# A hybrid encoder layer on one Trainium2 core: fewer accumulating bias transfers at the end, and earlier requests at the start of the last stage

## The chip, the cores and the metric

The kernel runs on one core of one Trainium2 chip. The metric is the device time of one execution in microseconds (us). Within the core, TensorE (PE in the profile) multiplies matrices, VectorE (DVE) and ScalarE (ACT) work elementwise, and GpSimd (POOL) and SyncE (SP) mostly ask for transfers. All transfers run on the same sixteen DMA engines.

## The reference

One layer over a sequence of 512 tokens of width 2048, in float32. The attention in the middle is not touched by the change; what follows it is.

```python
h = jnp.einsum('bsd,de->bse', x, w_in[layer])
qa, ka, va, ga, qb, kb, vb, gb = jnp.split(h, splits, axis=-1)
ya = _dilated_attention(heads(qa, N_HEADS_A), heads(ka, N_HEADS_A), heads(va, N_HEADS_A), t5_bias)
yb = _neighbourhood_attention(heads(qb, N_HEADS_B), heads(kb, N_HEADS_B), heads(vb, N_HEADS_B), na_rpb[layer])
ya = merge(ya) * jax.nn.silu(ga.astype(jnp.float32))
yb = merge(yb) * jax.nn.silu(gb.astype(jnp.float32))
y = jnp.concatenate([ya, yb], axis=-1).astype(x.dtype)
out = jnp.einsum('bse,ed->bsd', y, w_out[layer])
x = _layer_norm(DEEPNORM_ALPHA * x + out, ln_gain[layer], ln_bias[layer])
```

`_layer_norm` subtracts the mean over the 2048 columns, divides by the square root of the variance plus 1e-5, multiplies by the gain and adds the bias.

## The kernel before

Every float32 product is made of three matmuls: a high part (`wh`, made by ScalarE) and a low part (`wl`, the rest, made by VectorE) of the weights, and the same two parts of the data. The first two of the three use `wh`, the third `wl`.

The program has three stages. First the input projection in blocks. Then the attention over 32 heads in steps n = 0 to 131 (four steps a head): `scores`, an `exponent` on ScalarE, and two steps later `turn`, which transposes the probabilities p on TensorE and splits them into `th` (ScalarE) and `tl` (VectorE); `values` multiplies them with v. `fill` puts matmuls of the gates and of half the output projection between them. Last comes the rest of the output projection, as a list of 40 jobs, which `project(n)` works off. A job is twelve matmuls, mostly on one 128x1024 weight piece. `project(n)` also makes the high part (`high`, L898) and the low part (`low`, L903) of the weight of job n + 2, and runs the functions that `at(n, ...)` put down for job n, in the order in which they were put down. Jobs -2 and -1 are in steps 127 and 129 of the attention.

Some of the late products are arranged after Strassen. They need sums of quarters of y: `again(i)` asks in GpSimd's queue for pair i of y from DRAM (`ysum<-y_d`, L974), `combine_y(i)` forms the sums on VectorE (`csum`, L979 to L981), and `high_y` and `low_y` split them one and two jobs later. Two buffers serve in turn, so `again(i)` waits for `combine_y(i - 2)`; the two buffers held biases and probabilities of the heads before. The last pair of y goes through `rc_d` (denominators to DRAM), `rc` (back, spread over the partitions) and a product on VectorE (L779) before it is whole. Product 1 sums into `p1`, product 2 into `p2` and product 3 into `p3`, in the pools `pss` and `pst` of two PSUM banks each, which the attention used for its scores and its transposes.

`last_weight(u)` splits the four weight pieces of the last column block (`wlast`, L88 and L89), which jobs 36 and 38 and the matmuls behind the jobs use. The tokens are four rows t = 0 to 3 of 128, the columns four pieces i = 0 to 3 of 512. `norm(t)` normalises a row t < 3: `centre(i)` on VectorE (L1055) subtracts the mean and multiplies by the gain, `rescale(i)` on ScalarE (L1062) multiplies by the reciprocal root, an accumulating transfer in GpSimd's queue (`z<-in_lbias`, L1063) adds the bias, and SP stores the piece (`out<-z`, L1064) once that transfer has landed. Of the twelve pieces of these rows one (t = 2, i = 3) gets its bias on VectorE from a tile `bb[0]` instead (L1060). `last_norm` handles row 3, with the statistics' part of the shift made by small matmuls, and issues its stores (L1239) from ScalarE and SP in turn. Instructions of an engine and transfers of a queue start in the order in which they were recorded. The order is the program's own in these stages.

Of the kernel before, what the change touches and what calls it, by code (L numbers as in the profile page):

```python
# [9 lines left out]
AF = mybir.ActivationFunctionType  # L10
ALU = mybir.AluOpType
# [48 lines left out]
def _view(t, offset, dims):  # L60
    return bass.AP(tensor=t.tensor, offset=t.offset + offset, ap=dims)
# [10 lines left out]
def hybrid_layer(tc, xT, xn, w_in, w_early, w_mid, w_gate, w_out, t5x, brow, rpb, cmask, eye, gain, lbias, out):  # L72
    nc = tc.nc
    from contextlib import ExitStack
    with ExitStack() as ctx:
# [799 lines left out]
        def at(n, *fns):  # L875
            at_job.setdefault(n, []).extend(fns)

        def fetch(m):
            W[m] = slot(f"t{m % 4}", F32, "lraw") if m % 8 > 3 else raw_ring.next("lraw")
            nc.sync.dma_start(W[m], late_tiles[m])  # L880
# [91 lines left out]
        def again(i):  # L972
            cut_y[i] = yr.next("ysum")[:, :1024].rearrange("p (n q) -> p n q", n=4)
            nc.gpsimd.dma_start(cut_y[i].rearrange("p n q -> p (n q)"), y_d[i].rearrange("p n q -> p (n q)"))  # L974
# [49 lines left out]
            nc.scalar.activation(parts[name][t], acc[t], AF.Copy)  # L1024

        def gains():
            for tiles, src, first, some in ((gb, gain, 0, range(4)), (bb, lbias, 1, (3,))):
                for i in some:
                    t = slot(f"n{first + i}", F32, "gain")
                    nc.sync.dma_start(t, _view(src, 512 * i, [[0, 128], [1, 512]]))  # L1030
                    tiles.append(t)

        def last_weight(u):
            wts[u + 4] = [slot(f"r{2 * u + m}", F32R, "wlast") for m in range(2)]
            split(W[32 + u], *wts[u + 4])
# [12 lines left out]
        def norm(t):  # L1048
            mv = small.tile([128, 2], F32, name="mv", tag="mv")
            rs = small.tile([128, 1], F32, name="rs", tag="rs")  # L1050
            nm = small.tile([128, 1], F32, name="nm", tag="nm")

            def centre(i):
                zt = z[t][i]
                nc.vector.scalar_tensor_tensor(zt, zt, mv[:, 0:1], gb[i], op0=ALU.subtract, op1=ALU.mult)  # L1055

            def rescale(i):
                zt = z[t][i]
                if t == 2 and i == 3:
                    last.append(lambda: nc.vector.scalar_tensor_tensor(zt, zt, rs, bb[0], op0=ALU.mult, op1=ALU.add))  # L1060
                else:
                    nc.scalar.activation(zt, zt, AF.Copy, scale=rs)  # L1062
                    nc.gpsimd.dma_start(zt, _view(lbias, 512 * i, [[0, 128], [1, 512]]), accum_op=ALU.add)  # L1063
                last.append(lambda: nc.sync.dma_start(out[t * 128:t * 128 + 128, 512 * i:512 * i + 512], zt))  # L1064

            nc.vector.bn_aggr(mv, st[t])
            nc.scalar.activation(rs, mv[:, 1:2], AF.Sqrt, bias=eps)
            centre(1)
            nc.vector.reciprocal(rs, rs)
            rescale(1)  # L1070
            for i in (0, 2, 3):
                centre(i)
                rescale(i)
            while last and t < 2:
                last.pop(0)()

        def load_shift():

# [17 lines left out]
                    nc.sync.dma_start(f(rows[c][r:r + 1]), f(parts[:, at_ + 4 * c:at_ + 4 * c + 4]))  # L1096

        accs3, last = {}, []
        p1 = product(1, pss, 0)
        p2 = product(2, pst, 4)  # L1100
        o2 = second_half(2, 8)
        product(6, None, 12, p1)
        p5 = product(5, pacc, 16)
        product(7, None, 20, p1)
        p3 = product(3, pst, 24)
        product(4, None, 28, p1)
        for t in range(2):
            jobs.extend(((None, None, lambda w, t=t: third(t)), (None, None, lambda w: None)))
        for u in range(4):
            at(31 + u, lambda u=u: last_weight(u))  # L1110
        starts = (4, 6, 7, 9, 10, 12, 13, 14)
        for i, n in enumerate(starts):
            at(starts[i - 2] + 1 if i > 1 else 0, lambda i=i: again(i))
        for i, n in enumerate(starts):
            at(n, lambda i=i: combine_y(i))
            at(n + 1, lambda i=i: high_y(i))
# [36 lines left out]
        with tc.manual_schedule(engines=engines):  # L1153
            prepare()
            for _ in range(3):
                close()
            while step[0] < 0:
                fill(7)
                close()
            for n in range(132):  # L1160
                b, i = n % 4, n // 8
                mixing = n % 4 == 2 and 6 <= n <= 130
                amount = ((4, 5, 3, 5) if n < 80 else (4, 4, 3, 4))[b]
                if b == 0 and n < 124:
                    load_bias(n // 4 + 1)
                if n % 8 == 0 and n < 120:
                    load_kq(i + 1)
                if n % 8 == 4 and n < 128:
                    if n < 120:
                        load_v(i + 1)  # L1170
                    load_sg(i)
                exponent = scores(n) if n < 128 else None
                if mixing:
                    if exponent:
                        exponent()
                    behind_min(2)
                    fill(2)
                    mine, theirs, y, t = values(n // 4 - 1)
                    nc.scalar.activation(t, theirs, AF.Copy)
                    nc.vector.tensor_tensor(y, mine, t, ALU.add)  # L1180
                    fill(amount - 2)
                else:
                    fill(2)
                if 2 <= n < 130:
                    turn(n - 2)
                if b == 3:
                    behind_min(2 if len(held) > 3 and held[0][0] > 1 else 1)
                if not mixing:
                    if exponent:
                        exponent()  # L1190
                    fill(amount - 2)
                if n >= 8 and n % 8 == 0:
                    later(0, lambda i=i: nc.vector.reciprocal(dens[i - 1], dens[i - 1]))
                if n >= 8 and n % 8 == 2:
                    share(i - 1)
                if n >= 8 and n % 8 == 4:
                    later(0, lambda i=i: gate(i - 1), 4)
                if n % 8 == 1 and 2 <= i < 2 * PAIRS:
                    gated(i - 2)
                if n % 8 == 7 and i >= 2 * PAIRS - 1:  # L1200
                    gated(i - 1)
                if n >= 80 and n % 4 == 0 and n < 96:
                    load_x((n - 80) // 4)
                if n == 125:
                    while stream:
                        raws.append(raw_ring.next("wraw"))
                        nc.sync.dma_start(raws[-1], stream.pop(0))
                    W.update(enumerate(raws))
                    for m in range(4, 8):
                        fetch(m)  # L1210
                if n in (127, 129):
                    project((n - 131) // 2)
                close()
            fill(400)
            for n in range(len(jobs)):
                project(n)
        def last_norm(rows):
# [35 lines left out]
                nc.tensor.matmul(c, left[0:5], rows[i][0:5], start=True, stop=True)  # L1253
                shifts.append(c)
            centre(3)
            rescale(3, whole, bb[0])
            rescale(2, whole, shifts[0])
            rescale(0, whole, shifts[1])
            for part in (slice(0, 256), slice(256, 512)):
# [90 lines left out]
```

## Time and profile before

| | |
|---|---|
| median of three runs | 980.69 us (980.23 to 981.07) |
| profiled execution, its own time | 981.69 us |
| its span | 979.9 us, granted TensorE clock 0.994 |
| TensorE busy | 957.9 us of the span, 98% |
| VectorE, ScalarE, GpSimd busy | 797.3, 526.1, 234.6 us |
| DMA | 227.75 MB, mean 232 GB/s |
| accumulating bias transfers | 11 of 256 KB, 6.1 us each from issue to landing |
| first and last of them issued | 948.46 and 968.18 us |
| last arithmetic of VectorE ends | 967.40 us |

The span is what the profile covers; the execution's own time holds what lies around it. Times in the trace count from the span's start. Idle time of an engine costs something only where TensorE, or the end of the program, waits for it.

### The profile page before, as it was taken

The page shows a single profiled execution, that of the slowest core. Times are in us where ns is not written, and L with a number is a line of the kernel's source. Part 1 is how long each engine was busy: PE and PEld are TensorE (multiplying, and loading weights), DVE is VectorE, ACT ScalarE, POOL GpSimd, SP SyncE. Part 2 cuts the span into 40 slices and gives each one's busy share as a digit, 9 for nine tenths or more (in the row PEclk, how much of TensorE's full clock was granted, in tenths as well). Part 3 has the DMA queues.
Part 4 walks back from the last instruction along what each step waited for, and adds up shares of the span by engine and source line. Part 5 has one row for each costly group of instructions (what it writes and reads, how often), then busy time and mean ns, then how long its engine had stood idle before and what let it go on. Part 6 is the DMA issues. An engine that isn't in the chain of part 4 may idle for free.

```text
span 979.9 us, 14247 instructions
## 1 busy us (share of the span) xinstructions
PE 957.9 (98%) x4741; PEld 794.4 (81%) x4741; DVE 797.3 (81%) x1219; ACT 526.1 (54%) x900; POOL 234.6 (24%) x418
## 2 busy tenths in 40 slices
PE   8999999999999999999999999999999999999993
PEld 6878888888888889988888888888888778778873
DVE  7897778779789788897899857788878787799784
ACT  7454444444444344444445447777778777554531
POOL 1006646735645111111111100111111101210012
PEclk9999999999999999999999999999999999999997
DMA  9715797698496398743994887788879977677729
GB/s 334 275 65 133 224 322 215 179 292 234 113 361 205 106 345 252 248 172 127 287 254 170 260 274 244 239 257 270 264 233 282 322 254 236 223 249 231 253 36 255
DMA packets 131273, 227.75 MB, mean 232 GB/s; under 512 B 51247, under 2 KB 71599, under 8 KB 131200
## 3 DMA queue, kind: packets, MB, share of 16 engines
q1 hardware_dynamic: 109248, 174.93, 55.1%
q0 software_dynamic: 21232, 51.00, 17.8%
q10 hardware_dynamic: 720, 0.92, 0.3%
q8 instruction: 37, 0.61, 0.3%
q14 instruction: 36, 0.29, 0.1%
HBM read 169.66 MB, written 57.08 MB: 231 GB/s over the span
## 4 chain that ended last, share of the span: by engine, by line
PE 86%; issue 6%; DMA 3%; DVE 2%; ACT 1%; POOL 1%; POOLq 0%; SPq 0%; DVEq 0%; ACTq 0%
PE acc L405 16%; PE acc L407 16%; PE acc L406 16%; PE acc L601 9%; PE acc L924 5%; PE acc L807 5%; PE pt L726 3%; PE pv L748 3%; DMA rc_d<-tmp 2%; PE sc L707 2%; PE sc L706 2%; PE pt L262 1%; PE acc L281 1%; PE acc L283 1%; PE acc L282 1%
## 5 line engine op out<-in xcount | busy, mean ns | idle before, releaser
L378 ACT ACTIVATE wh<-braw 128x1024 fp32r<-128x1024 f32 x182 | 193.2, 1062 | 267.8 <-PE acc L406 198.2
L383 DVE TENSOR_TENSOR wl<-braw,wh 128x1024 fp32r<-128x1024 f32 x182 | 223.1, 1228 | 41.4 <-ACT wh L378 41.3
L405 PE MATMUL acc<-wh,xk 128*128 128x512 f32 x384 | 151.3, 394 | 0.0
L407 PE MATMUL acc<-wl,xk 128*128 128x512 f32 x384 | 149.7, 390 | 0.0
L406 PE MATMUL acc<-wh,xk 128*128 128x512 f32 x384 | 149.5, 389 | 0.0
L374 DVE TENSOR_TENSOR braw<-braw 128x1024 f32<-128x1024 f32 x104 | 127.6, 1227 | 0.1
L405 PE MATMUL acc<-wh,op 128*128 128x512 f32 x288 | 113.1, 393 | 0.0
L407 PE MATMUL acc<-wl,op 128*128 128x512 f32 x288 | 112.2, 390 | 0.0
L406 PE MATMUL acc<-wh,op 128*128 128x512 f32 x288 | 112.1, 389 | 0.0
L732 DVE TENSOR_TENSOR tl<-pt,th 128x256 fp32r<-128x256 f32 (+1 forms) x128 | 71.1, 555 | 25.1 <-ACT th L731 22.7
L405 PEld LDWEIGHTS acc<-wh,xk 128*128 128x128 f32 x384 | 72.1, 188 | 15.2 <-ACT bias L153 0.9
L407 PEld LDWEIGHTS acc<-wl,xk 128*128 128x128 f32 x384 | 72.1, 188 | 15.2
L406 PEld LDWEIGHTS acc<-wh,xk 128*128 128x128 f32 x384 | 72.2, 188 | 14.5
L601 PE MATMUL acc<-xk,wh 128*128 128x512 f32 x256 | 80.9, 407 | 0.0
L667 ACT ACTIVATE p<-s,mn 128x512 f32<-128x512 f32 (+1 forms) x96 | 62.4, 649 | 25.7 <-DVE mn L663 25.2
L663 DVE CUSTOM_DVE_ANT_0 s<-sc,biases 128x512 f32<-128x512 f32 (+2 forms) x128 | 67.7, 529 | 9.5 <-PE sc L707 8.8
L731 ACT ACTIVATE th<-pt 128x256 fp32r<-128x256 f32 (+1 forms) x128 | 62.2, 487 | 22.0 <-PE pt L726 19.8
L807 PE MATMUL acc<-wh,yk 128*128 128x512 f32 x192 | 67.8, 404 | 0.0
L163 POOL DMA_DIRECT2D bias<-rows_d x128 | 61.4, 487 | 16.4 <-DMA bias<-rows_d 6.4
L407 PEld LDWEIGHTS acc<-wl,op 128*128 128x128 f32 x288 | 54.1, 188 | 11.4
L406 PEld LDWEIGHTS acc<-wh,op 128*128 128x128 f32 x288 | 54.1, 188 | 11.0
L405 PEld LDWEIGHTS acc<-wh,op 128*128 128x128 f32 x288 | 54.1, 188 | 10.9
(202 smaller groups left out, 1878.9 us busy)
## 6 DMA issues: line engine op xcount, KB each, us to landing
braw<-in_w_in SPq DMA_DIRECT2D x96, 512.0 KB
k_d<-kst SPq DMA_DIRECT2D x64, 128.0 KB
q_d<-kst SPq DMA_DIRECT2D x64, 128.0 KB
v_d<-vst SPq DMA_DIRECT2D x32, 256.0 KB
wsum<-in_w_out POOLq DMA_DIRECT2D x32, 256.0 KB, 4.6
t_d<-wsum POOLq DMA_DIRECT2D x32, 256.0 KB, 3.2
q<-q_d SPq DMA_DIRECT2D x32, 256.0 KB
wraw<-in_w_gate SPq DMA_DIRECT2D x16, 512.0 KB
```

The source lines that it names most:

```text
L374: nc.vector.tensor_tensor(raws[q][u], raws[q][u], raws[other][u], ALU.add)
L378: nc.scalar.activation(h, raws[q][u], AF.Copy)
L383: nc.vector.tensor_tensor(l, raws[q][u], f(h), ALU.subtract)
L405: nc.tensor.matmul(accs[t], ah[:, q], h[:, c], start=first and k == 0, stop=False, skip_group_check=skip)
L406: nc.tensor.matmul(accs[t], al[:, q], h[:, c], start=False, stop=False, skip_group_check=skip)
L407: nc.tensor.matmul(accs[t], ah[:, q], l[:, c], start=False, stop=k == 7, skip_group_check=skip)
L601: nc.tensor.matmul(acc, w[:, k * 128:k * 128 + 128], X[8 * u + k][:, s], start=u == 0 and n == 0 and k == 0, stop=u == 1 and n == 2 and k ...
L663: nc.vector.tensor_tensor_reduce(*flat, bias, 1.0, 3e38, ALU.add, ALU.min, mn)
L667: nc.scalar.activation(p[:, to:to + n].rearrange("p (b r c) -> p b r c", r=8, c=c), s[:, :n].rearrange(order, r=8, c=c), AF.Exp, bias=mn, ...
L731: nc.scalar.activation(th, pt[:, :nch], AF.Copy)
L732: nc.vector.tensor_tensor(tl, pt[:, :nch], f(th), ALU.subtract)
L807: nc.tensor.matmul(acc[:, part], yk[k][:, t // 2, s, c], w[:, wk], start=first and kk == 0 and n == 0, stop=last and kk == 1 and n == 2)
```

## The change

It has five parts, all in the order or the place of work; the arithmetic is that of before.

1. Bias: piece 3 of rows 0, 1 and 2 and piece 2 of row 2 get it on VectorE, from two tiles `bb[0]` and `bb[1]`, the others by accumulating transfers, eight in place of eleven. In rows 0 and 1 the whole piece is stored first; in row 2 both are handled and stored in `last_norm`, as the one was before.
2. The stores of the other two pieces of row 2 go into GpSimd's queue instead of SP's.
3. The high parts of jobs 0 and 1 are made in steps 125 and 127 instead of 127 and 129; the low parts stay.
4. `again(0)` and `again(1)` are called in steps 127 and 130 instead of job 0; three of the eight combines are one job earlier; `p1` is in `pst`, and `p2` and `p3` in `pss`.
5. `last_weight` is called in jobs 30, 31, 34 and 35 instead of 31 to 34.

```diff
-            for tiles, src, first, some in ((gb, gain, 0, range(4)), (bb, lbias, 1, (3,))):
+            for tiles, src, first, some in ((gb, gain, 0, range(4)), (bb, lbias, 2, (2, 3))):
...
             def rescale(i):
                 zt = z[t][i]
-                if t == 2 and i == 3:
-                    last.append(lambda: nc.vector.scalar_tensor_tensor(zt, zt, rs, bb[0], op0=ALU.mult, op1=ALU.add))
-                else:
-                    nc.scalar.activation(zt, zt, AF.Copy, scale=rs)
-                    nc.gpsimd.dma_start(zt, _view(lbias, 512 * i, [[0, 128], [1, 512]]), accum_op=ALU.add)
-                last.append(lambda: nc.sync.dma_start(out[t * 128:t * 128 + 128, 512 * i:512 * i + 512], zt))
-
+                to = out[t * 128:t * 128 + 128, 512 * i:512 * i + 512]
+
+                def whole():
+                    nc.vector.scalar_tensor_tensor(zt, zt, rs, bb[max(i - 2, 0)], op0=ALU.mult, op1=ALU.add)
+                    nc.sync.dma_start(to, zt)
+
+                if i == 3 or t == 2 and i == 2:
+                    last.append(whole)
+                    return
+                nc.scalar.activation(zt, zt, AF.Copy, scale=rs)
+                nc.gpsimd.dma_start(zt, _view(lbias, 512 * i, [[0, 128], [1, 512]]), accum_op=ALU.add)
+                queue = nc.gpsimd if t == 2 else nc.sync
+                stores.append(lambda: queue.dma_start(to, zt))
...
             while last and t < 2:
-                last.pop(0)()
+                last.pop()()
+            for store in stores:
+                store()
...
-        p1 = product(1, pss, 0)
-        p2 = product(2, pst, 4)
+        p1 = product(1, pst, 0)
+        p2 = product(2, pss, 4)
...
-        p3 = product(3, pst, 24)
+        p3 = product(3, pss, 24)
...
-            at(31 + u, lambda u=u: last_weight(u))
-        starts = (4, 6, 7, 9, 10, 12, 13, 14)
-        for i, n in enumerate(starts):
-            at(starts[i - 2] + 1 if i > 1 else 0, lambda i=i: again(i))
+            at((30, 31, 34, 35)[u], lambda u=u: last_weight(u))
+        starts = (4, 5, 7, 8, 10, 11, 13, 14)
+        for i in range(2, 8):
+            at(starts[i - 2] + 1, lambda i=i: again(i))
...
+                if n == 130:
+                    again(1)
...
+                    first_high = jobs[0][0]()
                 if n in (127, 129):
-                    project((n - 131) // 2)
+                    ready_w.append(jobs[(n - 127) // 2][1](first_high))
+                    first_high = jobs[1][0]() if n == 127 else None
+                if n == 127:
+                    again(0)
+                if n == 129:
+                    for fn in at_job.pop(-1):
+                        fn()
...
-            rescale(3, whole, bb[0])
+            rescale(3, whole, bb[1])
```

In GpSimd's queue, at the last three heads (`rc_d` and `rc` are the denominators' way to DRAM and back, `y_d` the stores of y), the piece of the difference is:

```order
 L787 DMA y_d<-y 128x512
 L763 DMA rc<-rc_d 64x512 x2
+L974 DMA ysum<-y_d 128x1024 x2
 L767 DMA rc_d<-tmp 8x128
 L787 DMA y_d<-y 128x512
 L763 DMA rc<-rc_d 64x512 x2
-L974 DMA ysum<-y_d 128x1024 x3
+L974 DMA ysum<-y_d 128x1024
 L787 DMA y_d<-y 128x512
 L974 DMA ysum<-y_d 128x1024 x5
```

The first two requests for y stand ahead of the last pair's denominators instead of behind them.

On VectorE around job 30 (`wl` are low parts of the jobs' weights, `wlast` those of the last block, `z` and `st` sums and statistics of the rows):

```order
 L1012 BN_STATS st_5088<-z 128x6
 L903 TENSOR_TENSOR wl<-lraw,wh 128x1024
+L89 TENSOR_TENSOR wlast<-lraw,wlast 128x1024
 L814 SCALAR_TENSOR_TENSOR z<-xl,part 128x512
 L1009 TENSOR_TENSOR z<-acc,z 128x512
```

A `wlast` now stands ahead of the two sums, a statistic and the low part of job 32's weight, which follow it; it was behind that low part.

At the end of SP's queue, in the changed kernel (L1063 and L1071 are the stores of rows 0 to 2, L1258 those of row 3; `z` and `z_7235` to `z_7238` are tiles of the result):

```order
L1063 DMA out<-z_7235 128x512
L1071 DMA out<-z 128x512 x2
L1071 DMA out<-z_7235 128x512
L1063 DMA out<-z_7236 128x512
L1071 DMA out<-z 128x512 x2
L1071 DMA out<-z_7236 128x512
L1063 DMA out<-z_7237 128x512 x2
L1258 DMA out<-z_7238 128x512
L1258 DMA out<-z 128x256
```

Before, all twelve pieces of rows 0 to 2 stood there in the order of their rescaling, eleven of them behind a bias transfer of their own. Now six of ten are, and the two of row 2 that still have one follow their transfers in GpSimd's queue.

More of the change, by code (lines that the diff above doesn't have):

```diff
@@ L1058, in rescale @@
                 zt = z[t][i]
-                if t == 2 and i == 3:
-                    last.append(lambda: nc.vector.scalar_tensor_tensor(zt, zt, rs, bb[0], op0=ALU.mult, op1=ALU.add))
-                else:
-                    nc.scalar.activation(zt, zt, AF.Copy, scale=rs)
-                    nc.gpsimd.dma_start(zt, _view(lbias, 512 * i, [[0, 128], [1, 512]]), accum_op=ALU.add)
-                last.append(lambda: nc.sync.dma_start(out[t * 128:t * 128 + 128, 512 * i:512 * i + 512], zt))
+                to = out[t * 128:t * 128 + 128, 512 * i:512 * i + 512]
[9 more added lines that the diff above has]
+                stores.append(lambda: queue.dma_start(to, zt))
+            stores = []
             nc.vector.bn_aggr(mv, st[t])
```

## The prediction

> **What bounds the kernel now.** I read the page first: TensorE is busy 98% of the span, so only its few idle moments and the end after its last matmul can give time. Next come two stages of the end (columns: stretch, its length, then PE, PEld, DVE, ACT, POOL busy with counts, clock, DMA share, GB/s), and the DMA view of 948 to 979 us (q0 is GpSimd's, q1 SP's, q10 ScalarE's; packets, MB, share of sixteen engines).
>
> ```profile
> PE 957.9 (98%) x4741; PEld 794.4 (81%) x4741; DVE 797.3 (81%) x1219; ACT 526.1 (54%) x900; POOL 234.6 (24%) x418
> ...
> 956.00:960.00 4.00, 4.00 (x36) 4.00 (x35) 3.90 (x8) 2.11 (x4) 1.39 (x2) 1.00 1.05 257
> 968.00:972.00 4.00, 0.00 (x0) 0.00 (x0) 0.00 (x0) 0.00 (x0) 0.87 (x1) 0.58 1.05 276
> ...
> q0 software_dynamic: 1584, 2.88, 54.2%
> q1 hardware_dynamic: 2016, 3.54, 31.4%
> q10 hardware_dynamic: 432, 0.66, 5.8%
> z<-in_lbias POOLq DMA_DIRECT2D x11, 256.0 KB, 6.1
> ```
>
> After 968 no engine computes, but the DMA engines are full. Over these 31 us q0 carries only the eleven accumulating bias transfers: 0.542 x 31 / 11 = 1.53 us of all sixteen engines each. The other two carry the sixteen pieces of output: (0.314 + 0.058) x 31 / 16 = 0.72 us each. The sum, 11 x 1.53 + 16 x 0.72 = 28.4 us, is the whole stretch from about 950 to 978: the end is bound by DMA work, not by arithmetic.
>
> The waits of the queues and the timeline (start, length, engine, line; in brackets the idle time before and its releaser) show the order in it:
>
> ```profile
> DMA to landing us min/median/max: 4.5/6.1/6.4
> SPq L1064 <- DMA z<-in_lbias: 23.3, 11, 6.0
> ...
> 948.46 2.71 POOL L1063 DMA_DIRECT2D z<-in_lbias  x3 [71.78 <-ACT z L1062]
> 955.12 0.85 POOL L1063 DMA_DIRECT2D z<-in_lbias  x1 [0.99 <-ACT z L1062]
> 968.18 0.87 POOL L1063 DMA_DIRECT2D z<-in_lbias  x1 [1.62 <-issue]
> 975.28 1.19 SPq L1239 DMA_DIRECT2D out<-z  x2
> ...
> 947.19 2.06 DVE L1055 SCALAR_TENSOR_TENSOR z<-z,mv,gain 128x512 f32<-128x512 f32 x3
> 950.13 0.69 DVE L1009 TENSOR_TENSOR z<-acc,z 128x512 f32<-128x512 f32 x1 [0.89 <-PE acc L807]
> 962.46 0.68 DVE L1060 SCALAR_TENSOR_TENSOR z<-z,rs,gain 128x512 f32<-128x512 f32 x1
> 965.21 2.19 DVE L1236 SCALAR_TENSOR_TENSOR z<-z,rs,acc 128x512 f32<-128x512 f32 x4
> ```
>
> A bias transfer takes 6.1 us to land, about three are under way at once, so the last is asked for at 968.18. SP's stores stand behind them in order (23.3 us waited), and row 3's stores, ready at 965.21 + 2.19 = 967.40, leave SP only at 975.28 to 976.47. From there to the span's end are 3.4 us.
>
> Ahead of the end I read TensorE's waits and its timeline at the change of stage, and what VectorE waits for there.
>
> ```profile
> 834.92 0.38 PE L726 MATMUL pt<-ident,biases 128*128 128x128 f32 x2
> 837.18 0.62 PE L748 MATMUL pv<-tl,vv 128*128 128x256 f32 x3 [0.67 <-DVE tl L732]
> 837.66 0.70 PE L924 MATMUL acc<-wh,yk 128*128 128x512 f32 x2
> 839.64 0.74 PE L924 MATMUL acc<-wh,yk 128*128 128x512 f32 x2 [0.34 <-DVE y L1180]
> 841.13 0.62 PE L924 MATMUL acc<-wh,yk 128*128 128x512 f32 x2
> 854.73 0.61 PE L924 MATMUL acc<-wh,yk 128*128 128x512 f32 x2
> 855.97 0.50 PE L924 MATMUL acc<-wl,yk 128*128 128x512 f32 x1 [0.62 <-DVE wl L903]
> 858.40 0.62 PE L924 MATMUL acc<-wh,yk 128*128 128x512 f32 x2
> 858.86 0.39 PE L924 MATMUL acc<-wl,yk 128*128 128x512 f32 x1
> 861.13 0.61 PE L807 MATMUL acc<-wh,yk 128*128 128x512 f32 x2
> 862.36 0.50 PE L807 MATMUL acc<-wl,yk 128*128 128x512 f32 x1 [0.62 <-DVE wl L903]
> 936.66 0.50 PE L924 MATMUL acc<-wl,yk 128*128 128x512 f32 x1 [0.54 <-DVE wl L903]
> ...
> 834.09 1.04 ACT L898 ACTIVATE wh<-wraw 128x1024 fp32r<-128x1024 f32 x1
> 835.16 1.23 DVE L903 TENSOR_TENSOR wl<-wraw,wh 128x1024 fp32r<-128x1024 f32 x1 [1.23 <-ACT wh L898]
> 838.45 0.27 ACT L766 ACTIVATE tmp<-pt 8x128 f32<-8x128 f32 x1
> 844.64 7.90 DMA ysum<-y_d
> 852.57 0.69 DVE L979 TENSOR_TENSOR csum<-ysum 128x512 f32<-128x512 f32 x1 [3.71 <-DMA ysum<-y_d]
> 854.70 1.22 DVE L903 TENSOR_TENSOR wl<-lraw,wh 128x1024 fp32r<-128x1024 f32 x1
> ```
>
> An undisturbed job (twelve matmuls) takes 861.13 - 858.40 = 2.73 us, and its third matmul, the first to use the low weight, starts 0.46 in. Job 0 (837.66 to 841.13) took 3.47: 0.74 lost. Job 6 (854.73 to 858.40) took 3.67: 0.94 lost for a shown idle time of 0.62. Job 8 shows the same 0.62, so again 0.94; job 35 shows 0.08 less, so 0.86. The loss ahead of job 0 I put at its idle time, 0.7.
>
> **The change, part by part.**
>
> *First weights sooner.* VectorE idled 1.23 us for the high part of job 0's weight, which ScalarE began at 834.09. Now it stands two steps ahead, the low part follows at once, and the tl that TensorE waits for moves up. The moved 1.04 us is not free: it stands on ScalarE ahead of an exponent, and pushes the later th by some 0.2. I take 0.5 (ends 0 and 0.7). The second weight moves likewise, off the path.
>
> *p1's banks.* p1 changes pools with p2 and p3. Job 0's second bank is then freed by ScalarE's 0.27 us copy of the denominators instead of by VectorE's y, which ended just ahead of 839.64. That copy follows directly on the one that y itself waits for, so the bank is free before TensorE asks: 0.74 goes (ends 0 and 0.74).
>
> *y sooner.* The first two ysum requests, 512 KB each, go out when the last heads' probabilities are turned, the second behind 834.92; I estimate 834 and 835.5. In GpSimd's queue they pass rc_d and y_d of the last pair, whose source comes later on TensorE than what the requests wait for, so nothing behind them is held. At the 7.90 us that the first one took they land by 843.5; VectorE comes to them at 852.57 - 3.71 = 848.9. The 3.71 idle us vanish, the low weight of 854.70 ends near 852 instead, ahead of its use at 854.73 + 0.46, and the backlog that made job 8's weight late is gone too: 2 x 0.94 = 1.88 (ends 0 and 1.88). The combines in jobs 5, 8 and 11 instead of 6, 9 and 12 keep two jobs, 5.5 us, between request and use, and fit in the time won.
>
> *Last weights.* One of four splits moves from job 31 to 30, and two from 33 and 34 to 34 and 35.
>
> ```profile
> 921.85 1.06 ACT L898 ACTIVATE wh<-lraw 128x1024 fp32r<-128x1024 f32 x1 [1.18 <-PE acc L924]
> 923.89 1.21 DVE L903 TENSOR_TENSOR wl<-lraw,wh 128x1024 fp32r<-128x1024 f32 x1
> ```
>
> Job 35's 0.86 goes. But in job 30 VectorE now has the wlast first, which ScalarE can deliver only at 921.85 + 1.06 + 1.04 = 923.9. Behind it stand a put, an add and a statistic of the 0.69 kind, so job 32's wl, done at 925.1 before, ends at 923.9 + 1.2 + 2.1 + 1.2 = 928.4. Its use is due three jobs ahead of job 35's undelayed one: 936.66 - 0.7 - 3 x 2.73 = 927.8. A new loss of some 0.7 with its refill; net 0.2 gained (ends 0.86 gained and 0.4 lost).
>
> *The end.* Three of eleven bias transfers go: 3 x 1.53 = 4.6 us of DMA work. VectorE gets three operations of 0.68 to 0.75. In row 0 (947.19 + 2.06 = 949.25, next work at 950.13) and likewise in row 1 they fit into idle time. The third, ahead of row 3's chain (962.46), moves its end from 967.40 to 968.1, when the DMA engines still have work for some five microseconds: nothing, and 0.7 if that cover is gone. SP's queue no longer stands behind row 2's bias, so row 3's stores leave when VectorE is done. Two stores move to GpSimd's queue, where only their own transfers stand ahead; they carry the same bytes, 0.72 each. Do the engines stay full? By 964 the new order has issued 8 x 1.53 + 10 x 0.72 = 19.4 us of work against 14 elapsed: yes. The extra 256 KB of bias in job 24 joins loads of weights made eight jobs ahead: nothing, and 0.7 if they had no lead. Ends of this part: 2.1 (3 x 262144 bytes at 381 GB/s, the fastest slice among the last stores) and 5.5 (the 4.6 and small gaps between transfers). I take 4.6, because its row is that of these very transfers.
>
> Here the Trainium skill, page "DMA: Bandwidth & Descriptors", section "Anatomy of one DMA — SWDGE (gpsimd) path", prices the variable part of a transfer at its bytes over 436 GB/s. By it, as an estimate, one is 0.60 us, three are 1.8, and the sum would come out at 975.6. This trace's 1.53 us disagrees.
>
> Sum: 0.5 + 0.74 + 1.88 + 0.2 + 4.6 = 7.9 us. The profiled execution took 981.69 for its span of 979.9; the median of the three runs is 980.69, 0.8 over the span, and from it I subtract: **972.8 us**.
>
> **The rivals.**
> - *Only bytes count at the end:* the 1.53 is in part waiting inside packets, and three transfers bring 2.1. For it, the share passes 1.00; against it, the work adds up to the stretch. 980.69 - 3.3 - 2.1 = 975.3. The rule of the page above would be this rival's extreme.
> - *y is not sooner:* the early requests fall behind loads of weights, or ScalarE's moved weight takes back what it gives. Jobs 6 and 8 stay late: 972.8 + 1.9 = 974.7. Against it, even 7.90 us leaves five of slack.
> - *The change does hardly what it says:* both at once, and job 0 as before: 980.69 - 2.1 - 0.2 = 978.4.
> - *Slower, GpSimd's queue becomes the end.* Request 5 (955.12) makes room for request 8 by landing, and request 8 by landing frees the last store. With a landing time L the span is 955.12 + 2L + 0.6 + 0.87 + 3.4 - 3.3 = 956.7 + 2L: 968.9 at 6.1, not binding, and 976.3 at the longest landing of a ysum, the row below. It breaks even at L = 11.6 and is slower by 0.2% from 12.6; at 13 the median is 983.5. Against it, there is less traffic, not more.
>
> ```profile
> DMA to landing us min/median/max: 3.4/4.6/9.8
> ```
>
> The Trainium skill speaks for this one: "SBUF — State Buffer", section "SBUF: two separate sides", says that GpSimd can't write descriptors for its transfers while VectorE runs certain two-port operations. The issues of 0.85 and 0.87 us above, beside a VectorE busy 3.90 of 4 us, show no such hold.
>
> **How the numbers follow.** Chances: forecast 0.57 (own range 971.3 to 974.3, by the ends of the weights and job 0), only bytes 0.14, y not sooner 0.14, hardly 0.06, better than all these 0.04 (971, the ends of weights and of the tail), L between 10.6 and 12.6 0.03, above 0.02. Equal means within 0.2%, 978.7 to 982.7, about what a measurement of this kernel can tell from no change. So faster 0.95, same 0.03, slower 0.02. The range from 970.6 to 976.5 holds the forecast and both middle rivals with a microsecond about them.
>
> **What would show it.** The idle rows at ysum (3.71), tl, y and the wl of jobs 6 and 8 gone; a new wait of TensorE in job 32, none in 35; eight bias transfers at about 1.5 us of sixteen engines, the last asked for near 958; DMA share 1.0 until some five microseconds before the end; row 3's stores issued within a microsecond of VectorE's end. It would be wrong if the DMA share sank well before the end, or a GpSimd store landed last by far.

## The result, and the profile after

The median fell from 980.47 us (980.23 to 981.07, 4 runs) to 974.92 us (973.28 to 975.76, 4 runs): 5.55 us, a ratio of 0.9941 with a 95% interval of 0.9923 to 0.9958. A fourth run of the kernel before, 980.24, moved its median from the 980.69 of the first three. The change is faster by 0.6%, and the time lies in the predicted range, but 2.1 us above the 972.8 that the sum gave.

The profiled execution after the change took 974.88 us with a span of 973.1, so it is close to its median. That of before, on which the sum was built, took 981.69, a microsecond above its median. The page still says that TensorE is busy nearly throughout, now 956.4 us of a shorter span:

```profile
PE 956.4 (98%) x4741; PEld 794.0 (82%) x4741; DVE 799.8 (82%) x1222; ACT 523.7 (54%) x897; POOL 224.0 (23%) x417
```

**The end.** First the DMA view of 944 to 974 us (queue, packets, MB, share of sixteen engines), the windows (as in the prediction, length, engines, clock, DMA share, GB/s) and the waits of SP's queue:

```profile
q0 software_dynamic: 1312, 2.62, 45.5%
q1 hardware_dynamic: 1728, 3.02, 27.3%
q10 hardware_dynamic: 432, 0.66, 5.8%
z<-in_lbias POOLq DMA_DIRECT2D x8, 256.0 KB, 6.7
```

```profile
964.00:968.00 4.00, 0.00 (x0) 0.00 (x0) 0.99 (x3) 0.00 (x0) 1.14 (x2) 0.50 1.06 384
968.00:970.00 2.00, 0.00 (x0) 0.00 (x0) 0.00 (x0) 0.00 (x0) 0.00 (x0) 0.50 0.97 367
970.00:972.00 2.00, 0.00 (x0) 0.00 (x0) 0.00 (x0) 0.00 (x0) 0.00 (x0) 0.50 0.18 70
```

```profile
SPq L1071 <- DMA z<-in_lbias: 12.2, 6, 3.1
SPq L1364 <- DMA out<-z: 5.9, 1, 5.9
```

Fourteen pieces of output in the two hardware queues cost (0.273 + 0.058) x 30 / 14 = 0.71 us of all engines each. With the same price for GpSimd's two stores, its eight bias transfers cost (0.455 x 30 - 1.42) / 8 = 1.53 us each, as before. The engines are full until 970, and their last packets end near 970 + 2 x 0.18 = 970.4, yet the span runs on to 973.1: SP, at the very end, waits 5.9 us for one last store. The timeline shows which one it can be:

```profile
945.44 2.70 POOL L1069 DMA_DIRECT2D z<-in_lbias  x3 [74.05 <-ACT z L1068]
...
960.14 0.86 POOL L1069 DMA_DIRECT2D z<-in_lbias  x1 [2.67 <-ACT rs L1243]
...
962.81 2.18 DVE L1255 SCALAR_TENSOR_TENSOR z<-z,rs,acc 128x512 f32<-128x512 f32 x4
...
963.69 2.05 SPq L1258 DMA_DIRECT2D out<-z  x2
...
964.03 0.58 POOL L1071 DMA_DIRECT2D out<-z  x1 [3.04 <-DMA z<-in_lbias]
...
966.24 0.56 POOL L1071 DMA_DIRECT2D out<-z  x1 [1.63 <-DMA z<-in_lbias]
```

SP now issues row 3's stores at 963.69 to 965.74, when VectorE ends at 964.99. GpSimd asks for its last bias at 960.14, waits twice for such transfers to land, and puts the very last store out at 966.24. The answer for line 1071, which has these two stores of GpSimd, gives the time to landing:

```profile
DMA to landing us min/median/max: 5.4/5.7/6.1
```

So the last lands at 966.24 + 5.4 = 971.6 or later, when the engines have been empty for a microsecond.

**The start of the last stage, and the last weights.** The same timeline shows both requests of y early, VectorE without a wait at `csum`, and what happens ahead of jobs 0 and 32. The rows of TensorE at 836.57, 880.21 and 936.03 are the starts of jobs 0, 16 and 36:

```profile
833.32 0.58 POOL L974 DMA_DIRECT2D ysum<-y_d  x1
...
835.46 0.54 POOL L974 DMA_DIRECT2D ysum<-y_d  x1 [1.56 <-ACT th L731]
...
835.49 0.62 PE L748 MATMUL pv<-th,vv 128*128 128x256 f32 x3 [0.30 <-ACT th L731]
...
836.57 0.70 PE L924 MATMUL acc<-wh,yk 128*128 128x512 f32 x2
...
847.06 0.68 DVE L979 TENSOR_TENSOR csum<-ysum 128x512 f32<-128x512 f32 x1
...
880.21 0.62 PE L924 MATMUL acc<-wh,c 128*128 128x512 f32 x2
...
919.91 1.06 ACT L88 ACTIVATE wlast<-lraw 128x1024 fp32r<-128x1024 f32 x1 [0.58 <-DMA lraw<-in_w_out]
...
921.00 1.23 DVE L89 TENSOR_TENSOR wlast<-lraw,wlast 128x1024 fp32r<-128x1024 f32 x1 [2.68 <-ACT wlast L88]
...
925.46 0.50 PE L924 MATMUL acc<-wl,yk 128*128 128x512 f32 x1 [1.11 <-DVE wl L903]
...
936.03 2.20 PE L807 MATMUL acc<-wlast,yk 128*128 128x512 f32 x9
```

Ahead of job 0 TensorE's wait for `tl`, 0.67 us, is gone, and one of 0.30 for `th` has come. Jobs 0 to 15 take 880.21 - 836.57 = 43.64 us, 2.73 each, so nothing is lost in them. Job 32 loses more than predicted, because ScalarE waits 0.58 us for the first of the last weights (W[32] below). The chain of waits names its load, and what it follows:

```profile
904.45 6.85 DMA gain<-in_lbias
...
911.36 8.53 DMA lraw<-in_w_out
```

A table of such starts is the measure for what follows (us from each span's start; first bias is GpSimd's first accumulating request, end is the span's). 36 undisturbed jobs are 36 x 2.7275 = 98.2.

| kernel | job 0 | job 16 | job 36 | first bias | end | jobs 0-15 | jobs 0-35 | from job 36 |
|---|---|---|---|---|---|---|---|---|
| before | 837.66 | 883.80 | 939.05 | 948.46 | 979.9 | 46.14 | 101.39 | 40.85 |
| before again (E5) | 837.50 | 883.23 | 938.48 | 947.89 | 979.2 | 45.73 | 100.98 | 40.72 |
| after | 836.57 | 880.21 | 936.03 | 945.44 | 973.1 | 43.64 | 99.46 | 37.07 |
| early parts alone (E1) | 836.84 | 880.47 | 935.73 | 945.14 | 977.8 | 43.63 | 98.89 | 42.07 |
| end alone (E2) | 836.62 | 880.89 | 936.17 | 945.58 | 973.5 | 44.27 | 99.55 | 37.33 |
| y alone (E11) | 837.58 | 881.85 | 937.11 | 946.53 | 978.5 | 44.27 | 99.53 | 41.39 |
| weights and banks alone (E12) | 836.07 | 880.22 | 935.50 | 944.92 | 978.0 | 44.15 | 99.43 | 42.50 |

Between the profiles of before and after, 6.8 us of span: 1.1 came ahead of job 0, 2.5 in jobs 0 to 15, -0.57 in jobs 16 to 35, and 3.8 from job 36 on.

### The profile page after: what moved, and what is told of

Its sections match the earlier page's. It is cut to its first block, busy times and chain, and to the rows that moved or that the text cites. A ratio compares the mean times of both kernels' runs of the same rounds, so it can differ in the third digit from the quotient of the medians.

```text
span 973.1 us, 14243 instructions
## 1 busy us (share of the span) xinstructions
PE 956.4 (98%) x4741; PEld 794.0 (82%) x4741; DVE 799.8 (82%) x1222; ACT 523.7 (54%) x897; POOL 224.0 (23%) x417
## 4 chain that ended last, share of the span: by engine, by line
PE 91%; DMA 2%; ACT 2%; issue 2%; DVE 1%; POOL 0%; SPq 0%; POOLq 0%; ACTq 0%; DVEq 0%
PE acc L405 16%; PE acc L407 16%; PE acc L406 16%; PE acc L601 9%; PE acc L807 7%; PE acc L924 6%; PE pv L748 4%; PE pt L726 4%; PE sc L707 2%; PE sc L706 2%; PE pt L262 1%; PE acc L281 1%; PE acc L282 1%; PE acc L283 1%; PE acc L398 1%
```

## The experiments

The edits are given in short: lines that only follow from those shown, such as the added loads of bias, are left out. Line numbers in a profile are those of its own kernel. Ratios are to the kernel before, with 95% intervals; times of before moved between 980.28 and 981.22 from one set of runs to another.

**E1 and E2: the two halves.** E1 is the kernel before with only the early edits (first weights, y, banks); E2 is the kernel before with only the bias and the stores.

```diff
# E1, on before
+ first_high = jobs[0][0]()                # n = 125; low parts at 127, 129
+ again(0) at n = 127, again(1) at n = 130; starts = (4, 5, 7, 8, 10, 11, 13, 14)
+ p1 = product(1, pst, 0); p2 = product(2, pss, 4); p3 = product(3, pss, 24)
# E2, on before
+ rescale: pieces 3 of rows 0 to 2 and piece 2 of row 2 on VectorE; row 2's stores from GpSimd
```

> The kernel before with the early part alone: first weights two steps sooner, the first two requests for y in steps 127 and 130, the three combines one job earlier, p1's pool; the end and the last weights as before. Theory: TensorE loses nothing more at tl, y and the low weights of jobs 6 and 8, and the shift reaches the end unchanged, since the end's DMA work is asked for as much sooner: 3.1 us, about 977.4 us, and job 35's wait (0.54 idle) still there. Rival, the gain is swallowed at the end because the end's DMA work is the limit from a point that does not move: 980 us or more.

> The kernel before with the end alone: eight bias transfers instead of eleven and row 2's two stores in GpSimd's queue. Theory: three times 1.53 us of DMA work gone, less about 1 us because the store in GpSimd's queue lands last and late: 3.6 us, about 976.9 us; the last DMA packets end some 4.6 us sooner against job 36 than before. Rival, only bytes count: 2.1 us, 978.4 us.

E1 took 978.37 us (977.68 to 981.73), ratio 0.9982 [0.9972, 0.9991]: some 1.8 us faster where 3.1 were in the sum. E2 took 975.53 (974.55 to 976.6), ratio 0.995 [0.9938, 0.9962], some 4.9. So the end carries most of the gain, and the early edits brought less than their sum. E2 gained more than the 3.6 expected of it, but not all of that at the end: its profile is 6.4 us shorter than that of before, of which 3.5 come from job 36 on. The other 2.9 came ahead of job 36, where its code is that of before up to one more load of bias. In E2's profile, whose early code is that of before, no low weight is late in jobs 6 and 8 (jobs 0 to 15 take 44.27: only job 0's 0.7 is lost). That put the 1.88 of y in doubt.

**E5: before, profiled again.**

> The kernel before, profiled a second time. Asked: is the stall of jobs 6 and 8, which the prediction took for 1.88 us, in every execution? Theory (it hangs on how long the first ysum takes to land, and that varies): with a landing under 6 us the idle 3.71 us of VectorE at ysum shrinks below 2, no wait for a low weight stands in jobs 6 and 8, and job 0 to job 16 take about 44 us instead of 46.1. Rival (it is part of every execution): the two waits of 0.62 us stand again, and job 0 to job 16 take 46 us. The span should be 979 to 980 either way.

It took 980.93. The waits of TensorE in it name the low weights again (a part of the first row is job 35's), and VectorE's timeline shows why:

```profile
PE acc L924 <- DVE wl L903: 0.7, 2, 0.6
PE acc L807 <- DVE wl L903: 0.6, 1, 0.6
```

```profile
851.96 0.69 DVE L979 TENSOR_TENSOR csum<-ysum 128x512 f32<-128x512 f32 x1 [3.24 <-DMA ysum<-y_d]
```

The stall is there again, as the rival said, with 45.73 us for jobs 0 to 15, 0.4 less than in the first profile. The landing under 6 us that the theory wanted was not met here, but E2 met it. Its row reads:

```profile
849.01 0.69 DVE L979 TENSOR_TENSOR csum<-ysum 128x512 f32<-128x512 f32 x1 [1.19 <-DMA ysum<-y_d]
```

There the first ysum, asked for at 843.45, was there 5.5 us later; in the prediction's row it took 7.90. At 5.5 us nothing of the wait reaches TensorE.

**E11 and E12: the early half taken apart.** E11 is before with y alone sooner, E12 with the first weights and the banks alone.

```diff
# E11, on before
+ again(0) at n = 127, again(1) at n = 130; starts = (4, 5, 7, 8, 10, 11, 13, 14)
# E12, on before
+ first_high = jobs[0][0]()                # n = 125; low parts at 127, 129
+ p1 = product(1, pst, 0); p2 = product(2, pss, 4); p3 = product(3, pss, 24)
```

> The kernel before with y alone asked for sooner (first two ysum requests among the last heads, combines one job earlier); weights, banks and the end as before. The prediction's 1.88 for jobs 6 and 8. Theory: the stall stands in most executions of the kernel before (in both of its profiles, 1.9 and 1.5 us), so job 0 to job 16 take 44.3 us (16 x 2.72 and job 0's 0.74) and the time falls by 1.5 to 1.9, to about 979.0 beside 980.6. Rival: it is an accident of some executions, as its absence in the profile with the end alone changed lets one think; the time falls by under 0.8 us.

> The kernel before with the first weights sooner and p1's banks exchanged alone; y and the end as before. The prediction's 0.5 + 0.74. Theory: job 0 starts some 0.5 sooner and loses nothing, the two waits for low weights in jobs 6 and 8 stand as before (job 0 to job 16 about 45.4), and the time falls by 1.2 to about 979.4 beside 980.6. Rival: TensorE, sooner in job 0, waits the longer for the same y in job 6 and job 8, since the landing of ysum sets their time: job 0 to job 16 take 46 us or more and the time falls by under 0.6 us.

E11 took 980.38 us (979.59 to 981.68, 11 runs), ratio 0.9996 [0.9987, 1.0006]: no change that can be told from none, at most 1.3 us. Its jobs 0 to 15 took the 44.27 that the theory said, and the time did what the rival said. E12 took 979.17 (977.78 to 979.96, 11 runs), ratio 0.9982 [0.9973, 0.9991], 1.8 us, above the 1.2 expected. Its rival's place showed faintly: one late low weight in job 8,

```profile
PE acc L807 <- DVE wl L903: 0.2, 1, 0.2
```

and jobs 0 to 15 took 44.15, half a microsecond above the undisturbed 43.6. So four profiles with y asked for late show 1.9, 1.5, 0 and 0.5 us of that stall. A mean near 1 explains some half of what E11 lacks. The rest went at the end: from the first bias request to the end of the span it took 31.4 and 31.3 in the two profiles of before, but 32.0, 33.1 and 32.7 in E11, E12 and E1, which came there sooner. So the rival of E1, a gain swallowed at the end, holds in part. Two differences stand in the traces. In E1 and E12 the share of GpSimd's queue gives 1.59 us for a transfer, in E11 1.58, against 1.53 and 1.57 in the two of before. And in E11 and E12 the DMA engines, full until then, run short just ahead of row 3's stores (40 slices of 946 to 979 and of 944 to 979 us, busy tenths):

```profile
DMA  0029698999999999999999999999999944999100
...
DMA  0009599999999999989999999999999725997000
```

From 972 to 974 in E11 and from 971 to 974 in E12 they lose 0.9 and 1.2 us, beside 0.4 in the first profile of before and nothing in the second. SP issues those stores at 973.87 and 973.35, right behind the last stores that wait for a bias. E1 has no such gap, so the two do not account for all of it, and why the same transfers took longer was not settled.

**E3 and E6: the last weights.** E3 is the changed kernel with the four splits back in jobs 31 to 34. E6 leaves them as changed, and loads the extra row of bias in job 33 instead of 24.

```diff
# E3
-            at((30, 31, 34, 35)[u], lambda u=u: last_weight(u))
+            at(31 + u, lambda u=u: last_weight(u))
# E6
-  (bb, lbias, 2, (2, 3))
+  (bb, lbias, 1, (3,))
+        at(33, lambda: late_bias(2))
```

> The changed kernel with the last weights split in jobs 31 to 34 as before. Theory: the wait of job 32 (1.11 us idle, about 1.26 lost) goes and job 35's (0.86 lost) comes back: 0.4 us faster than the changed kernel, about 974.5 us, no difference within its noise. Rival, moving the weights was right and brings what it was priced at: 0.2 to 0.9 us slower than the changed kernel. TensorE's wait rows for the low weight in jobs 32 and 35 decide, more than the time.

> The changed kernel, but the extra row of bias (256 KB) is loaded in job 33 instead of in job 24. Theory: job 32's wait has two parts, the order on VectorE that the prediction priced at 0.7, and 0.58 us that ScalarE waits for W[32]'s load, which runs behind the extra bias; with the bias gone from there the load lands in under 8 us, ScalarE waits for nothing, and TensorE's wait in job 32 falls from 1.1 to about 0.5. About 974.4, 0.5 less than the changed kernel's 974.92. Rival (the order alone): the wait stays at 1.0 or above and the time at 974.9.

E3 took 974.26 (973.29 to 975.0), ratio 0.9936 [0.9924, 0.9948]; E6 974.11 (972.98 to 974.96), ratio 0.9937 [0.9924, 0.9951]. Both medians are below the 974.92 of the change, by less than the intervals' width, so the profiles decide. In E3 job 32 waits for nothing and job 35's wait is back:

```profile
932.54 0.50 PE L924 MATMUL acc<-wl,yk 128*128 128x512 f32 x1 [0.53 <-DVE wl L903]
```

In E6 the wait of job 32 is down from 1.1 to 0.4, and ScalarE's split of the first last weight no longer waits for its load:

```profile
PE acc L924 <- DVE wl L903: 0.4, 1, 0.4
```

```profile
918.22 1.04 ACT L88 ACTIVATE wlast<-lraw 128x1024 fp32r<-128x1024 f32 x1
```

Jobs 0 to 35 take 99.46 in the changed kernel, 98.89 in E3 (836.05 to 934.94) and 98.75 in E6 (835.57 to 934.32). Against 98.2 that is a loss of 1.27, 0.70 and 0.56. So in these profiles the order on VectorE costs 0.56, near the 0.7 predicted, the late load of W[32] the other 0.71, and job 35's old loss was 0.70. But that load is not late in every execution. With the order of the change and the bias in job 24, job 32 waits 1.1 us after the change and 1.5 in E4, but only 0.4 in E10, where ScalarE waits for no load:

```profile
918.43 1.04 ACT L88 ACTIVATE wlast<-lraw 128x1024 fp32r<-128x1024 f32 x1
```

With the bias out of job 24 the wait is 0.4 in all three profiles that have this order (E6, E7, E8). So the extra bias can cost up to a microsecond, and in one profile of three it cost nothing.

**E4: row 2's stores.** The changed kernel, with those two stores in SP's queue behind all of row 3's.

```diff
-                queue = nc.gpsimd if t == 2 else nc.sync
+                queue = nc.sync
+            if t == 2:
+                behind_all.extend(stores)    # issued at the end of last_norm
+                return
```

> The changed kernel with row 2's two stores behind a bias transfer issued by SP behind all of row 3's instead of by GpSimd. Theory: in the changed kernel the second of these stores is asked for at 966.24 and lands last, about 972, 2.8 us ahead of which the packets have ended; from SP the same store lands with the others, so the span shrinks by 0.5 to 1.2 us, about 974 us. Rival, the end is set by the DMA engines' total work whoever asks: no difference, 974.9 us.

It took 973.97 us (973.58 to 974.3), ratio 0.9933 [0.9921, 0.9945], though job 32 waits 1.5 us in it. From job 36 it takes 972.1 - 936.00 = 36.1 us, 1.0 less than after. The two stores leave SP late, and yet the waits at the end are short:

```profile
966.05 0.88 SPq L1071 DMA_DIRECT2D out<-z  x2
```

```profile
SPq L1369 <- DMA out<-z: 3.8, 6, 1.8
```

The longest wait for a store is 1.8 us instead of 5.9. The packets end hardly sooner than after the change, near 970 + 2.1 x 0.11 = 970.2 beside 970.4:

```profile
970.00:972.10 2.10, 0.00 (x0) 0.00 (x0) 0.00 (x0) 0.00 (x0) 0.00 (x0) 0.50 0.11 40
```

Job 36 starts at 936.00 here and at 936.03 after the change, so the times can be compared directly: the last store is issued at 966.6 (the second of the two, 0.33 us of issue each), 0.4 later than GpSimd's, and the span ends 1.0 earlier, all but 0.2 of it behind the last packets. In this pair of profiles the place of the store cost about a microsecond, as the expectation had it; the medians differ by as much, 0.95, but their runs overlap.

**E8: row 2 without transfers.** The changed kernel with row 2's last two bias transfers on VectorE too, three more rows of bias held in SBUF and loaded in job 33, and row 2's stores from SP.

```diff
-                if i == 3 or t == 2 and i == 2:
+                if i == 3 or t == 2:
                     last.append(whole)
```

> The changed kernel with row 2's last two accumulating transfers also done by VectorE (ahead of row 3's chain), all of its stores from SP; three more rows of bias loaded in job 33. Theory (DMA work): 2 x 1.53 = 3.1 us of work less, VectorE's end 2 x 0.68 = 1.4 later (966.4); total 6 x 1.53 + 16 x 0.72 = 20.7 us from about 949.5: drained at 970.2 at the earliest, span about 971, time 972 to 973. Rival (the end is VectorE's chain and a landing, the transfers are hidden by then): 1.4 us later, 976.

It took 971.74 (970.88 to 972.15), ratio 0.9908 [0.9895, 0.9922]; the span is 970.2. Of the 3.2 us under the change, 0.65 came in jobs 0 to 35 (836.91 to 935.72), where the bias is not loaded in job 24 any more. From job 36 it takes 34.5, 1.6 less than E4, whose row 2 is also stored by SP. That is half of two transfers' 3.1 us, because the bound passes to VectorE: its chain ends at 964.02 + 2.19 = 966.2, and the windows show that the DMA engines first run short and then fill again with the last stores:

```profile
960.00:964.00 4.00, 1.10 (x4) 0.79 (x4) 3.76 (x9) 0.27 (x1) 0.00 (x0) 0.86 0.75 272
964.00:968.00 4.00, 0.83 (x2) 0.11 (x1) 2.19 (x4) 0.00 (x0) 0.00 (x0) 0.50 1.02 379
968.00:970.00 2.00, 0.00 (x0) 0.00 (x0) 0.00 (x0) 0.00 (x0) 0.00 (x0) 0.50 0.30 101
```

**E10: the transfer without accumulating.** The changed kernel with its eight bias transfers writing over z, so that the normalised row is not in the output; a measurement of the price.

```diff
-  nc.gpsimd.dma_start(zt, ..., accum_op=ALU.add)
+  nc.gpsimd.dma_start(zt, ...)
```

> The changed kernel with its eight bias transfers writing the bias over z instead of accumulating onto it (the bias is not added to the normalised row: a measurement of the transfer alone). Theory: the 1.53 us of all sixteen engines is the price of accumulating; a plain transfer of the same rows costs about the 0.72 us of a store, so 8 x 0.8 = 6.5 us of DMA work go, the share of the DMA engines falls clearly below 1 between 952 and 964, and the end is VectorE's or the last GpSimd store: time 970.5 to 972.5. Rival: the price is that of GpSimd's queue or of the source, one row read for 128 partitions; 1.5 us stays and the time is 974.9.

970.88 us (970.28 to 971.54), ratio 0.99 [0.9885, 0.9915]. The DMA view of its 943 to 969 us:

```profile
q0 software_dynamic: 800, 2.62, 36.8%
q1 hardware_dynamic: 1728, 3.02, 30.7%
q10 hardware_dynamic: 432, 0.66, 6.8%
z<-in_lbias POOLq DMA_DIRECT2D x8, 256.0 KB, 5.5
```

A piece of output takes (0.307 + 0.068) x 26 / 14 = 0.70 us, so a plain bias transfer takes (0.368 x 26 - 1.39) / 8 = 1.02. Accumulating costs 0.5 of the 1.53, a third; the theory had put it at 0.8. From job 36 the run takes 968.5 - 934.57 = 33.9 us, 3.1 less than after. An accumulating transfer has 1584 / 11 = 144 packets (in the row of before), a plain one of the same queue 800 / 10 = 80; but a store in the hardware queues has 2160 / 14 = 154, so the number of packets alone does not set the price. The remaining 0.3 above a store belongs to the queue or to the source, one row read for 128 partitions; which of the two was not tried.

**E7: the additions on GpSimd.** The changed kernel with its eight transfers replaced by additions on GpSimd from bias rows in SBUF, row 2's stores from SP.

```diff
-  nc.gpsimd.dma_start(zt, ..., accum_op=ALU.add)
+  nc.gpsimd.tensor_tensor(zt, zt, bb[3 - i], ALU.add)
```

> The changed kernel with all eight accumulating bias transfers replaced by additions on GpSimd from bias rows held in SBUF (three more rows loaded in job 33), and row 2's stores in SP's queue. Theory (the end is DMA work, 1.53 us for each accumulating transfer): 8 x 1.53 = 12.2 us of work go, the DMA engines drain long before VectorE is done, and the end is VectorE's (965.0 in the changed kernel's profile) and one lightly loaded landing of 2 to 3 us with issue: span 968.5 to 970, time 970 to 972. GpSimd's additions I estimate at 2.1 us each from its 1.95 us for 128x480, so the eighth ends near 962. Rival: GpSimd beside VectorE slows VectorE, whose own chain has only 0.4 us of idle time left; with its 1 us per row or more the time is 974 or above.

973.51 us (973.03 to 973.75), ratio 0.9927 [0.9913, 0.994]: the rival's mechanism, at a little less than its price. In its timeline VectorE's three centrings take 3.09 us and its bias 1.66 while GpSimd adds:

```profile
943.63 3.09 DVE L1060 SCALAR_TENSOR_TENSOR z<-z,mv,gain 128x512 f32<-128x512 f32 x3
...
944.56 5.01 POOL L1074 TENSOR_TENSOR z<-z,late_bias 128x512 f32<-128x512 f32 x3 [73.19 <-ACT z L1073]
...
946.76 1.66 DVE L1067 SCALAR_TENSOR_TENSOR z<-z,rs,gain 128x512 f32<-128x512 f32 x1
...
948.35 0.68 DVE L1009 TENSOR_TENSOR z<-acc,z 128x512 f32<-128x512 f32 x1
...
966.61 2.19 DVE L1262 SCALAR_TENSOR_TENSOR z<-z,rs,acc 128x512 f32<-128x512 f32 x4 [0.23 <-PE acc L1279]
```

In the changed kernel the same two groups take:

```profile
944.16 2.06 DVE L1055 SCALAR_TENSOR_TENSOR z<-z,mv,gain 128x512 f32<-128x512 f32 x3
...
946.26 0.75 DVE L1062 SCALAR_TENSOR_TENSOR z<-z,rs,gain 128x512 f32<-128x512 f32 x1
```

VectorE loses 1.9 us in row 0 and as much in row 1, and ends at 968.8 instead of 965.0. The median is 1.4 us under that of the change, where the theory had 3 to 5.

**E9: the best of these.** E8 with the last weights split in jobs 31, 32, 34 and 35.

```diff
-            at((30, 31, 34, 35)[u], lambda u=u: last_weight(u))
+            at((31, 32, 34, 35)[u], lambda u=u: last_weight(u))
```

> The version with row 2's bias on VectorE, and the last weights split in jobs 31, 32, 34 and 35 instead of 30, 31, 34 and 35. Theory: job 32's wait (0.4 there, 0.7 with its refill) goes since VectorE has no early weight ahead of job 32's, job 35's does not come back since only one split stands in job 34, and the end, which is VectorE's chain behind TensorE's last matmuls, moves forward by as much: 971.74 - 0.7 = 971.0. Rival: the split that is now later makes another low weight late, in job 33 or 34, by as much: 971.7.

970.73 us (970.1 to 971.5), ratio 0.9896 [0.988, 0.9913]: faster than both kernels. Its chain of waits runs through TensorE without a step aside from job 16 to the last product:

```profile
880.81 54.42 PE acc L924 x240
935.23 19.19 PE acc L807 x96
954.42 2.90 PE sc L807 x24
```

Jobs 0 to 35 take 935.07 - 837.02 = 98.05, nothing lost. Behind TensorE the chain holds VectorE's work for rows 2 and 3, until 965.4; then come the last stores, to the end of the span at 969.7.

## Why the prediction was right, and where it was not

Direction, range and place were right: most of the gain is in the transfers of the end. The sum of 7.9 was 2.4 too high, and three of its five terms were off. The time lies outside the 971.3 to 974.3 that the forecast gave itself; it is the wide range, made to hold the rivals too, that covers it.

- *First weights 0.5 and p1's banks 0.74.* E12 brought 1.8 for both, with an interval of 0.9 to 2.6, which holds the 1.24. The time of job 0's start does not show the 0.5, because it lies anywhere from 835.57 (E6) to 837.02 (E9) where its weights are early. TensorE's wait ahead of it does: 0.67 for `tl` became 0.30 for `th`, 0.4 less. The new wait lies on ScalarE, where the prediction had put a cost of 0.2. The banks' wait is gone.
- *y sooner 1.88: the step that failed most.* The mechanism is as described, and in the profiled execution the 1.9 us did come back. The error was to take the stall of one execution for that of all: the run's own time was a microsecond above the median, the stall hangs on a landing of 5.5 to 7.9 us, and four profiles show 1.9, 1.5, 0 and 0.5. The sum also let every early microsecond through to the end, and with the old end E11, E12 and E1 lost 0.6 to 1.7 of them there. Alone the edit brought 0.4 us, and at most 1.3; E1, which has it, and E12, which has all of E1 but it, both brought 1.8.
- *Last weights +0.2.* In the profiled execution they cost 0.57. Job 35's loss went (0.70 for the predicted 0.86) and the order on VectorE cost 0.56 for the predicted 0.7. What failed is a sentence in another part: that the extra bias in job 24 "joins loads of weights made eight jobs ahead: nothing". The load of W[32] was issued when that bias had landed, at 904.45 + 6.85 = 911.30, took 8.53 us, and made job 32 lose 0.71 more. Without that bias (E6, E7, E8) this loss does not stand; with it it stands in two profiles of three (E10 has none). Where it is absent, the moved weights gain 0.70 - 0.56 = 0.14, near the predicted 0.2.
- *The end, 4.6.* The price was right: 1.53 us in the profile of the change, 1.53 to 1.69 in all. In E4, whose eight transfers are as in the change, the end is 40.85 - 36.1 = 4.75 us shorter. In the changed kernel it is 3.8, because the last store stands in GpSimd's queue and ends the program a microsecond later than E4's. The prediction had counted the stores' bytes alone, and named such a landing only as what would make it wrong. The estimate of 0.60 from the Trainium skill, "DMA: Bandwidth & Descriptors", section "Anatomy of one DMA — SWDGE (gpsimd) path", fits neither the accumulating transfer nor E10's plain one, 1.02.
- *Rivals.* "Only bytes count" fell with E4, E8 and E10. "y not sooner" met the time, 974.7 beside 974.92, but not the mechanism: in the profile y was sooner. "GpSimd's queue becomes the end" was the right place with a small price: the request at 960.14 was held back 2.7 us and the last store was last, by 1 us. That the request waited for a landing is argued: the profile names a ScalarE result that it does not use. The Trainium skill's hold of GpSimd's descriptors ("SBUF — State Buffer", section "SBUF: two separate sides") did not show: issues beside the busy VectorE took 0.84 to 0.88 us, as before. (Of the two issues that the prediction names, the one at 968.18 stood beside an idle VectorE; its 0.87 is the price without a hold.)
- *What would show it.* Gone, as listed: the idle rows at ysum, `tl` and `y`, and the late weights of jobs 6, 8 and 35. (VectorE waits 1.5 us at a later `csum`, at 860.99, and no weight is late for it.) Seen: the wait in job 32, the full DMA engines, row 3's stores within a microsecond of VectorE's end. Not as listed: the engines are full until three microseconds before the end, not five, and the last bias is asked for at 960.14, not near 958.

## What to carry to other kernels

A stall that hangs on the landing of a transfer is worth what it costs over several executions; look at how far the profiled run lies from its median, and profile the kernel before twice. When a load is added "with nothing waiting for it", name the next transfer in its queue and who waits for that one. At an end that is bound by DMA work, price each transfer by its share of the engines, take work from it until another engine's chain is the bound, and try the last store in another queue than GpSimd's, which cost a microsecond here.

## What the runs showed of the hardware

- A 256 KB bias transfer took 1.53 to 1.59 us of sixteen engines when it accumulated (before, after, E1), and 0.375 x 27 / 6 = 1.69 at the most (E9, 943 to 970 us); it took 1.02 when it wrote (E10), and a store of 256 KB 0.70 to 0.72.
- A GpSimd addition holds up VectorE on operands in SBUF. The addition of 128x512 takes 5.01 / 3 = 1.67 us, and a VectorE operation of 0.75 us took 1.66 beside it (E7); whether the addition is longer for it was not tried. The Trainium skill, "SBUF — State Buffer", section "SBUF: two separate sides", says that the two share a pair of ports, which one instruction holds whole while the other waits when a VectorE operation with two SBUF inputs meets a GpSimd operation that reads SBUF. The trace agrees: the VectorE operation became as long as a GpSimd one. The operation that reads `acc` (in PSUM) kept its 0.68 us beside the addition, in the row of 948.35.
- Issued on full DMA engines, the two stores from GpSimd's queue took 5.4 and 6.1 us to land; with the last store in SP's queue, issued 0.4 us later, the program ended 1.0 sooner (after and E4).
